# A two-layer hybrid block on one core: the later modulation tiles of layer 0 formed by TensorE in column groups

## The chip, the core and the metric

The kernel runs on one core of one Trainium2 chip. The metric is the device time of one execution in microseconds (us). The profile names the engines PE (TensorE, matmuls; PEld is its loading of weights), DVE (VectorE), ACT (ScalarE), POOL (GpSimd) and SP (SyncE, which issues all of this kernel's DMAs from one queue).

## The reference

Two layers over 512 image tokens and 256 context tokens of 1024 channels, all in float32. A condition vector c (and c_ctx for the context tokens) gives, by one matrix per layer, six vectors of 1024 channels: shift, scale and gate of the mixers, shift, scale and gate of the MLP.

```python
cond = jax.nn.silu(c)
cond_ctx = jax.nn.silu(c_ctx)
for i in range(DEPTH):
    mod = (cond @ mod_w[i] + mod_b[i])[:, None, :]
    mod_c = cond_ctx @ mod_w[i] + mod_b[i]
    sh1, sc1, g1, sh2, sc2, g2 = jnp.split(mod, 6, axis=-1)
    ...
    u = modulate(rmsnorm(h, norm1_g[i]), sh1, sc1) @ w_in[i]
    ...   # four mixers: SSD scan, differential attention, grouped-query attention, latent attention
    h = h + g1 * (jnp.concatenate([y_a, y_b, y_c, y_d], axis=-1) @ w_out[i])
    h = h + g2 * squared_relu_mlp(modulate(rmsnorm(h, norm2_g[i]), sh2, sc2), mlp_w1[i], mlp_w2[i])
    ...   # in layer 0 the same for the context tokens, with mod_c
return rmsnorm(h, final_norm_g)
```

mod_w[i] is 1024 x 6144, so a layer's modulation is 48 tiles of 128 channels, each the product of a 1024 x 128 block with two vectors.

## The kernel before

Channels lie on the partitions and tokens along the free dimension. Every large product is made of three matmuls (high by high, high by low, low by high), as activations and weights are split into exact pairs of 12-bit parts: ACT copies the high part and DVE or POOL forms the low part (`split`, L346 to L349).

The modulation is formed in two ways. Tiles 0 to 15 of layer 0 (shift and scale of the first norm) are formed at the start on PE: `mod_load` (L260 to L272) has the two condition vectors as stationary columns, padded with zeros to 32 (`sil`), and moves 256 columns of the weights past them. The eight blocks of the contraction go to four groups of 32 PSUM partitions, two blocks to a group; `mod_done` (L274) then adds the groups and turns channels onto the partitions by four matmuls against the 0/1 matrix `sel`. All later tiles, 16 to 47 of layer 0 and all 48 of layer 1, are formed on DVE by `mod_block` (L295 to L307): two loads of 128 x 512 with a column of the matrix on each partition, four (in layer 1's later tiles two) multiplies with a running sum against the condition vectors spread over all partitions (`cb`), whose product goes to `junk` and whose sum is kept (L305), and a last instruction that adds halves and bias (L307).

A layer has two stages. `mixers` (from L647) runs five tracks side by side: attention, support (all projections, then the preparation of latent attention), the SSD scan, modulation (`mods`, tiles 16 to 39 in layer 0: first gate, second shift and scale), and the first part of the out projection. A table of costs and weights (`Weave`, `TUNE`) decides which track writes its next step into the program; each engine then works off its instructions in the order that results from it. After the mixers come the rest of the out projection and the MLP, where `next_mod` hangs a tile on each of the first eight up projections (tiles 40 to 47, the MLP's gate, from `mod_now`) and later layer 1's 48 tiles.

What the change shares with the rest: the loads of weights and of modulation columns rotate through seven buffers (tag `wr`); all small PSUM results (transposes, side projections, sums) rotate through four banks (tag `g`), scores through two larger ones (`S`); the SSD scan has three buffers under the tag `sd`.

Of the kernel before, what the change touches and what calls it, by code (L numbers as in the profile page):

```python
# [19 lines left out]
P = 128  # L20
D = 1024
KT = 8
# [8 lines left out]
# columns of w_in by 128-wide tile, in the order in which the kernel names them  # L31
# [27 lines left out]
# parameter columns of a layer  # L59
# [12 lines left out]
class Weave:  # L72
    """Runs generators side by side. A track is (generator, weight); a generator yields the cost of its last
    step, or None while it cannot go on, and the track whose weighted cost is least goes next."""
# [45 lines left out]
def hybrid_block_kernel(ctx: ExitStack, tc: tile.TileContext, a: dict, out: bass.AP, dbg=None):  # L120
# [8 lines left out]
    # how the tracks of a layer are woven: costs of hops between engines and through DMA, weights, priorities  # L129
# [98 lines left out]
    # silu(c), silu(c_ctx) as zero-padded stationary columns  # L228
# [6 lines left out]
    sil = sd("sil", (P, KT, 32))  # L235
# [24 lines left out]
    def mod_load(i):  # L260
        """shift and scale of two channel tiles on TensorE, four contraction tiles side by side, for the first norm"""
        po = ps_o(f"pm{i}")
        for j in range(2):
            for k0 in range(0, KT, 3):
                n = min(3, KT - k0)
                w = mws.pop((i, j, k0))
                for k in range(k0, k0 + n):
                    g = k % 4
                    mm(po[32 * g : 32 * g + 32, 256 * j : 256 * j + 256], sil[:, k], w[:, k - k0], start=k < 4, stop=k >= 4)
        m = sd(f"ms{i}", (P, 512))  # L270
        act(m, po, AF.Copy)
        return m  # L272
# [10 lines left out]
    cb = const("cb", [P, 2, D])     # silu(c), silu(c_ctx) on every partition  # L283
# [9 lines left out]
    junk = const("junk", [P, 512], mybir.dt.bfloat16)  # L293

    def mod_block(l, c):  # L295
        """a column of mod_w on each partition"""
        L = lay[l]
        n = 2 if l + 1 < DEPTH or c < MG1 else 1
        m = tiny(f"ma{l}_{c}", 4)
        for i in range(2):  # L300
            w = sb.tile([P, 512], F32, name=f"mv{l}_{c}_{i}", tag="wr", bufs=NWR)
            half = slice(512 * i, 512 * i + 512)
            ld(w, a["modw"][l, c, :, half])
            for s in range(n):
                stt(out=junk, in0=w, scalar=1.0, in1=cb[:, s, half], op0=ALU.mult, op1=ALU.mult,  # L305
                    accum_out=m[:, 2 * i + s : 2 * i + s + 1])
        stt(out=L.mod[:, c, 0:n], in0=m[:, 0:n], scalar=col(L.v, V_MODB + c), in1=m[:, 2 : 2 + n], op0=ALU.add, op1=ALU.add)  # L307

    LO0 = nc.gpsimd.scalar_tensor_tensor
    LOP = ()  # L310

    def mod_gain(l, which, k0, k1):
        """gain * (1 + scale) for channel tiles k0..k1"""
        L = lay[l]
        off, voff = (MSC1, V_N1) if which == 1 else (MSC2, V_N2)
        key = f"gs{l}_{which}"
        if not hasattr(L, key):
            setattr(L, key, const(key, [P, KT, 2]))
        g = getattr(L, key)
        n = 2 if which == 1 or l + 1 < DEPTH else 1  # L320
        stt(out=g[:, k0:k1, 0:n], in0=L.mod[:, off + k0 : off + k1, 0:n], scalar=1.0,
            in1=L.v[:, voff + k0 : voff + k1].unsqueeze(2).to_broadcast([P, k1 - k0, n]), op0=ALU.add, op1=ALU.mult)
        return g

# [1 line left out]
    def rstd(name, srcs, parts, r):  # L326
        """srcs: (squares / count [K, tokens], 0/1 weights [K, P]) whose products add up to the mean squares.
        r <- 1 / sqrt(mean + eps) on every row that the mean is for."""
        for i, s in enumerate(parts):
            ps = ps_r(f"{name}_ms{i}")[:, 0 : s.stop - s.start]  # L330
            for j, (x, w) in enumerate(srcs):
                mm(ps, w, x[:, s], start=j == 0, stop=j == len(srcs) - 1)
            yield K.hop
            yield from rstd_of(f"{name}_q{i}", ps, r, s)

    def rstd_of(name, ps, r, s):
# [3 lines left out]
        # one Newton step  # L340
# [5 lines left out]
    def split(hi, lo, src, sub=tt):  # L346
        """fp32 -> an exact pair of 12-bit parts."""
        act(hi, src, AF.Copy)  # L348
        sub(out=lo, in0=src, in1=f(hi), op=ALU.subtract)  # L349

    def weights(name, src, m, sub=tt):
        """src: [P, k-tiles * m], a block of columns in k-tiles, or two blocks; loaded, then split by halves.
        A generator: loads, first half, second half; returns the (hi, lo) operands"""
# [19 lines left out]
    def gemm(outs, w, xs):  # L373
        """outs: (PSUM view, token slice)"""
# [8 lines left out]
    def big_gemm(name, w, xs, toks, evac, m=P):  # L383
        """x and context in one PSUM tile of two banks; evac(view, tokens)"""
        ps = ps_s(name)
        b = toks[0].start
        yield from gemm([(ps[0:m, t.start - b : t.stop - b], t) for t in toks], w, xs)
        evac(ps[0:m, 0 : toks[-1].stop - b], slice(b, toks[-1].stop))

    def side_gemm(name, w, xs, toks, evac, m=P):  # L390
        """one bank, one token range after the other"""
# [15 lines left out]
    def pump(gap):  # L407
        """a step of the deferred work, every `gap` steps"""
# [9 lines left out]
    def ahead(jobs, at=(0, 0)):  # L418
        """jobs: (weights, use); the weights of the next job are asked for before the use of this one,
        and their halves split after the steps `at` of it"""  # L420
# [41 lines left out]
    def norm_part(name, h, acc, gain, shift, si, s, xn):  # L462
        """rmsnorm over all channels, modulated, split, for the tokens s"""
# [6 lines left out]
    def squares(name, acc, k, h, s, add=gtt):  # L470
        """acc += h * h / D"""
# [7 lines left out]
    def sigmoid_of(t):  # L479
        """t <- 1/(1+exp(-t)), t >= -80"""  # L480
# [38 lines left out]
    def v_start(l):  # L519
        """V of diff and gqa, tokens on partitions"""  # L520
# [56 lines left out]
    # 0/1 matrices that add up the rows of a head: two heads of 64 rows, four of 32 rows, two of 32 + 32 rows  # L577
# [35 lines left out]
    def rope32(x, rows, name):  # L613
        """rotates 32-row groups in place on the image tokens"""
# [11 lines left out]
    def mixers(l, xn, yd, h, ys):  # L626
# [63 lines left out]
        class Unit:  # L690
            """one head and query tile on its way through the softmax"""
# [33 lines left out]
        def pv(us, vcols):  # L725
            """two heads side by side: out [(head, dim), query]"""
# [9 lines left out]
        def attend(begin, rest, middle, vcols, store, s_cost, lag=1):  # L736
            """two heads, in three stages over the (query tile, head) units: scores and softmax, transposed, times V"""
# [18 lines left out]
        def finish(i, yo):  # L756
            """parks an output until the out projection"""
# [71 lines left out]
        def gnorm(name, xs_, w, count, gains, parts):  # L829
            """xs_: (rows, tile)"""  # L830
# [160 lines left out]
        def ssd_dt():  # L991
# [3 lines left out]
            dts = mid(f"dts{l}", 48, 7)   # softplus(dt + bias)  [token, (d, t, h)]  # L995
# [8 lines left out]
            # log1p(e) = 2 atanh(e / (2 + e)), e = exp(-|x|)  # L1004
# [28 lines left out]
            wst = mid(f"wst{l}", 48, 7)   # dt * exp(acs_end - acs)  # L1033
# [5 lines left out]
            nb = mid(f"nb{l}", 48, 7)     # ln(dt) - acs  # L1039
# [5 lines left out]
        def conv(name, i):  # L1045
            """centred convolution of width 3 from PSUM, silu"""
# [159 lines left out]
        def modjobs():  # L1206
            if l == 0:
                for c in range(MG1, MG2):
                    yield c

# [24 lines left out]
        def mods():  # L1235
            for c in modjobs():
                mod_block(l, c)
                yield K.w_m
            done.add("mods")

# [34 lines left out]
    for l in range(DEPTH):  # L1275
# [24 lines left out]
        def out2_jobs(si, s):  # L1300
            """the contraction tiles of mla, four output tiles at a time"""
# [15 lines left out]
        mod_now = iter(range(MG2, 48) if l == 0 else ())  # L1317
        mod_next = iter(range(48) if l + 1 < DEPTH else ())

        def next_mod(g):  # L1320
            if g == 0:
                c = next(mod_now, None)
                if c is not None:
                    mod_block(l, c)
# [103 lines left out]
def _layout(i):  # L1428
    """The inputs as the kernel loads them: copies and permutations only."""
    i = {n: np.asarray(v) for n, v in i.items()}  # L1430

    def cols(v):            # channels -> [P, tiles]
        return v.reshape(-1, P).T

    def rep(v):             # one row on every partition
        return np.broadcast_to(v.reshape(1, -1), (P, v.size))

    def ktiles(w):          # [K, n] -> [P, k-tiles, n]
        return w.reshape(-1, P, w.shape[1]).transpose(1, 0, 2)

    def blocks(w):          # [1024, n * P] -> [n, P, KT * P]
# [18 lines left out]
    for l in range(DEPTH):  # L1460
# [10 lines left out]
         "rope": _rope_tables(), "win": np.stack(win), "wv": np.stack(wv), "modw": np.stack(modw), "mod0": i["mod_w"][0][:, 0 : 2 * D].reshape(KT, P, 2, 4, 256).transpose(3, 2, 1, 0, 4),  # L1471
# [19 lines left out]
```

## Time and profile before

| | us |
|---|---|
| median of 3 runs (1855.38 to 1856.95) | 1855.81 |
| span of the profiled execution, first to last instruction | 1851.9 |
| PE busy | 1743.4 |
| DVE busy | 1188.5 |
| ACT busy | 870.0 |
| POOL busy | 536.6 |

The page gives the busy time of each engine over the whole span, 29429 instructions. It is an average over stages with different limits: the start (to about 56 us), layer 0's mixers (to about 460), its out projection and MLP (to about 1093), and the same for layer 1. The rows below are therefore taken by stretches of the span. Busy time of PE runs to the modelled end of each matmul, so matmuls that stand alone take more of it than matmuls in a dense row.

### The profile page before, as it was taken

The page shows a single profiled execution, that of the slowest core. Times are in us where ns is not written, and L with a number is a line of the kernel's source. Part 1 is how long each engine was busy: PE and PEld are TensorE (multiplying, and loading weights), DVE is VectorE, ACT ScalarE, POOL GpSimd, SP SyncE. Part 2 cuts the span into 40 slices and gives each one's busy share as a digit, 9 for nine tenths or more (in the row PEclk, how much of TensorE's full clock was granted, in tenths as well). Part 3 has the DMA queues.
Part 4 walks back from the last instruction along what each step waited for, and adds up shares of the span by engine and source line. Part 5 has one row for each costly group of instructions (what it writes and reads, how often), then busy time and mean ns, then how long its engine had stood idle before and what let it go on. Part 6 is the DMA issues. An engine that isn't in the chain of part 4 may idle for free.

```text
span 1851.9 us, 29429 instructions
## 1 busy us (share of the span) xinstructions
PE 1743.4 (94%) x10686; PEld 1467.2 (79%) x10686; DVE 1188.5 (64%) x2352; ACT 870.0 (47%) x1768; POOL 536.6 (29%) x477
## 2 busy tenths in 40 slices
PE   7979888899988999999999999998999999999996
PEld 5967677677777988888888889786778998888885
DVE  5799998877499964543543164877976863333324
ACT  5345656777354313213213353676877752323242
POOL 2443552220235201001002664465211320101065
PEclk9989899999999999999999999999999999999998
DMA  8465331013344642442433434422014552323233
GB/s 329 128 177 170 91 103 39 10 52 142 96 143 148 199 131 93 146 132 92 150 123 95 135 113 121 128 73 66 13 48 161 169 162 95 97 92 98 94 121 98
DMA packets 117328, 216.23 MB, mean 117 GB/s; under 512 B 15424, under 2 KB 24640, under 8 KB 117184
## 3 DMA queue, kind: packets, MB, share of 16 engines
q1 hardware_dynamic: 117184, 214.36, 37.4%
q8 instruction: 84, 1.38, 0.3%
q14 instruction: 60, 0.49, 0.1%
HBM read 185.99 MB, written 8.13 MB: 105 GB/s over the span
## 4 chain that ended last, share of the span: by engine, by line
PE 64%; DVE 17%; issue 5%; POOL 4%; ACT 4%; DMA 3%; SPq 3%; DVEq 0%; POOLq 0%; ACTq 0%
PE p L380 41%; DVE junk L305 4%; PE po L380 3%; SPq L673 2%; PE pv L530 2%; PE pr L380 2%; PE m_s L701 2%; PE m_o L732 2%; PE m_t L722 1%; DMA mv<-in_modw_dram 1%; DVE d_m L706 1%; POOL w_512s L349 1%; DVE d_p L785 1%; PE pdk L380 1%; DVE hs L1116 1%
## 5 line engine op out<-in xcount | busy, mean ns | idle before, releaser
L348 ACT ACTIVATE w_0s<-w 128x512 fp32r<-128x512 f32 x256 | 160.8, 630 | 389.8 <-PE p L380 370.3
L305 DVE SCALAR_TENSOR_TENSOR junk<-mv,cb 128x512 bf16<-128x512 f32 x256 | 200.9, 785 | 129.0 <-DMA mv<-in_modw_dram 126.4
L1345 POOL TENSOR_TENSOR r<-r 128x512 f32<-128x512 f32 (+2 forms) x80 | 92.0, 1152 | 648.8 <-ACT a_0h L1344 310.5
L349 DVE TENSOR_TENSOR w_0s<-w,w_0s 128x512 fp32r<-128x512 f32 x216 | 151.5, 703 | 158.2 <-ACT w_0s L348 157.9
L1269 DVE SCALAR_TENSOR_TENSOR h<-p,modT,h 128x512 f32<-128x512 f32 (+1 forms) x104 | 62.6, 623 | 101.1 <-PE p L380 101.1
L1343 ACT ACTIVATE r<-p 128x512 f32<-128x512 f32 (+2 forms) x80 | 47.7, 596 | 156.5 <-PE p L380 153.8
L710 ACT ACTIVATE d_p<-d_s,d_m 128x768 f32<-128x768 f32 (+1 forms) x80 | 65.0, 815 | 66.5 <-DVE d_m L706 62.5
L779 POOL TENSOR_TENSOR d_p<-d_p,d_m 128x768 f32<-128x768 f32 (+1 forms) x40 | 59.1, 1478 | 85.8 <-DVE d_m L714 83.7
L706 DVE TENSOR_REDUCE d_m<-d_s 128x1 f32<-128x768 f32 (+1 forms) x80 | 66.0, 840 | 4.6 <-PE d_s L701 4.4
L349 POOL TENSOR_TENSOR w_0s<-w,w_0s 128x512 fp32r<-128x512 f32 x40 | 55.1, 1388 | 41.0 <-ACT w_0s L348 37.9
L477 POOL TENSOR_TENSOR acc<-acc,sq 128x256 f32<-128x256 f32 (+1 forms) x48 | 49.2, 1026 | 46.4 <-ACT sq L476 40.3
L701 PE MATMUL d_s<-sdk,sdq 128*128 128x256 f32 (+1 forms) x144 | 43.7, 391 | 18.5 <-ACT d_p L710 12.0
L380 PE MATMUL p<-xm_0h,w_0s 128*128 128x512 f32 (+1 forms) x176 | 54.4, 355 | 2.5 <-ACT r L1343 2.2
L380 PE MATMUL p<-a_0h,w_0s 128*128 128x512 f32 (+1 forms) x176 | 54.4, 355 | 0.9 <-DVE h L1269 0.5
L380 PE MATMUL p<-xm_4h,w_0s 128*128 128x512 f32 (+1 forms) x176 | 54.4, 356 | 0.5 <-DVE w_0s L349 0.5
L380 PE MATMUL p<-xm_5h,w_0s 128*128 128x512 f32 (+1 forms) x176 | 54.4, 355 | 0.0
L380 PE MATMUL p<-xm_3h,w_0s 128*128 128x512 f32 (+1 forms) x176 | 54.4, 355 | 0.0
L380 PE MATMUL p<-a_4h,w_0s 128*128 128x512 f32 (+1 forms) x176 | 54.4, 354 | 0.0
L380 PE MATMUL p<-xm_2h,w_0s 128*128 128x512 f32 (+1 forms) x176 | 54.4, 355 | 0.0
L380 PE MATMUL p<-xm_1h,w_0s 128*128 128x512 f32 (+1 forms) x176 | 54.3, 355 | 0.0
L380 PE MATMUL p<-xm_6h,w_0s 128*128 128x512 f32 (+1 forms) x176 | 54.3, 355 | 0.0
L380 PE MATMUL p<-a_2h,w_0s 128*128 128x512 f32 (+1 forms) x176 | 54.1, 354 | 0.0
(2374 smaller groups left out, 5659.4 us busy)
## 6 DMA issues: line engine op xcount, KB each, us to landing
w<-in_w_dram SPq DMA_DIRECT2D x320, 256.0 KB, 2.7
mv<-in_modw_dram SPq DMA_DIRECT2D x160, 256.0 KB, 2.9
wr<-in_wout_dram SPq DMA_DIRECT2D x32, 256.0 KB, 2.8
h<-in_xT_dram SPq DMA_DIRECT2D x16, 384.0 KB, 6.9
mw<-in_mod_dram SPq DMA_DIRECT2D x16, 384.0 KB, 6.1
wo<-in_wout_dram SPq DMA_DIRECT2D x32, 192.0 KB, 2.5
wv<-in_wv_dram SPq DMA_DIRECT2D x16, 192.0 KB, 4.7
y<-yd SPq DMA_DIRECT2D x6, 384.0 KB, 4.0
```

The costliest lines, as they stand in the source:

```text
L305: stt(out=junk, in0=w, scalar=1.0, in1=cb[:, s, half], op0=ALU.mult, op1=ALU.mult, accum_out=m[:, 2 * i + s : 2 * i + s + 1])
L348: act(hi, src, AF.Copy)
L349: sub(out=lo, in0=src, in1=f(hi), op=ALU.subtract)
L380: mm(o, w[k][wi], xs[k][xi][0:r, t], start=k == 0 and wi == 0 and xi == 0, stop=k == n - 1 and wi == 1)
L477: (tt if k == KT - 1 else add)(out=acc[:, s], in0=acc[:, s], in1=q[:, s], op=ALU.add)
L701: mm(u.ps[:, b:e_], q[:, P * t : P * t + P], k[:, u.k0 + b : u.k0 + e_], start=i == 0, stop=i == len(passes) - 1)
L706: nc.vector.tensor_reduce(out=u.m[:, 0:1], in_=u.ps[:, 0 : u.n], axis=AX.X, op=ALU.max, negate=True)
L710: act(u.p, u.ps[:, 0 : u.n], AF.Exp, bias=u.m[:, 0:1], accum_out=u.m[:, 1:2])
L779: gtt(out=a.p, in0=a.p, in1=a.r.to_broadcast([P, n]), op=ALU.mult)
L1269: stt(out=h[k][:, s], in0=ps, scalar=L.mod[:, mg + k, si : si + 1], in1=h[k][:, s], op0=ALU.mult, op1=ALU.add)
L1343: act(r, ps, AF.Relu)
L1345: gtt(out=r, in0=r, in1=r, op=ALU.mult)
```

## The change

The 32 later tiles of layer 0 are formed on PE as the first 16 are, four tiles at a time (`mod_quad`). A tile is two loads (the same 2 x 256 KB, another layout of the same numbers), eight matmul calls with 32 stationary and 128 moving columns into four groups of partitions of one small PSUM bank, and one copy by ACT; after four tiles four matmuls against `sel` add the groups, and one DVE instruction adds the bias for the four. `sil` gets a buffer of its own, as it now lives on; `junk` moves to the ring `sc` of two buffers. Layer 1's tiles stay with `mod_block`.

```diff
-    sil = sd("sil", (P, KT, 32))
+    sil = const("sil", [P, KT, 32])
...
-    junk = const("junk", [P, 512], mybir.dt.bfloat16)
...
+        junk = sb.tile([P, 512], mybir.dt.bfloat16, name=f"junk{l}_{c}", tag="sc", bufs=NSC)
...
+    def mod_quad(c0):
+
+        L = lay[0]
+        m = sd(f"mq{c0}", (P, 512))
+        for j in range(4):
+            ws = []
+            for i in range(2):
+                w = sb.tile([P, 4, P], F32, name=f"mk{c0 + j}_{i}", tag="wr", bufs=NWR)
+                ld(w, a["modk"][c0 + j - MG1, :, 4 * i : 4 * i + 4])
+                ws.append(w)
+            po = ps_g(f"pk{c0 + j}")
+            for k in range(KT):
+                g = k % 4
+                mm(po[32 * g : 32 * g + 32, 0:P], sil[:, k], ws[k // 4][:, g], start=k < 4, stop=k >= 4)
+            act(m[:, P * j : P * j + P], po[:, 0:P], AF.Copy)
+            yield K.w_m
+        pq = ps_g(f"pl{c0}")
+        for j in range(4):
+            mm(pq[:, 2 * j : 2 * j + 2], m[:, P * j : P * j + P], sel, start=True, stop=True)
+        tt(out=L.mod[:, c0 : c0 + 4], in0=pq[:, 0:8].rearrange("p (k s) -> p k s", s=2),
+           in1=L.v[:, V_MODB + c0 : V_MODB + c0 + 4].unsqueeze(2).to_broadcast([P, 4, 2]), op=ALU.add)
...
         def mods():
-            for c in modjobs():
-                mod_block(l, c)
-                yield K.w_m
+            if l == 0:
+                for c in range(MG1, MG2, 4):
+                    yield from mod_quad(c)
             done.add("mods")
...
-        mod_now = iter(range(MG2, 48) if l == 0 else ())
+        mod_now = (x for c in ((MG2, MG2 + 4) if l == 0 else ()) for x in mod_quad(c))
...
             if g == 0:
-                c = next(mod_now, None)
-                if c is not None:
-                    mod_block(l, c)
+                next(mod_now, None)
```

The order of the instructions follows from the tracks, so some of it moves. On DVE, where differential attention's first units begin (d_..._m are the row maxima and sums of a unit, dq the rotated queries), there stood before:

```order
L714 RECIPROCAL d_0_0_1_0_m<-d_0_0_1_0_m 128x1 [waits Activation_49]
L305 SCALAR_TENSOR_TENSOR junk,ma_21_988<-mv_21_1_993,cb 128x512 [waits DMAHW7_49]
L706 TENSOR_REDUCE d_0_0_1_1_m<-d_0_0_1_1_s 128x1 [waits PE_49]
L706 TENSOR_REDUCE d_0_1_0_0_m<-d_0_1_0_0_s 128x1 [waits PE_49]
L621 TENSOR_TENSOR dq_1106<-dq_1106,rddq_1_1195 128x512 [waits DVE_49,Pool_49]
L305 SCALAR_TENSOR_TENSOR junk,ma_21_988<-mv_21_1_993,cb 128x512 [waits DVE_49]
L714 RECIPROCAL d_0_0_1_1_m<-d_0_0_1_1_m 128x1 [waits Activation_49]
```

Now the same place has the unit's work alone:

```order
L735 RECIPROCAL d_0_0_1_0_m<-d_0_0_1_0_m 128x1 [waits Activation_49]
L727 TENSOR_REDUCE d_0_1_0_0_m<-d_0_1_0_0_s 128x1 [waits PE_49]
L642 TENSOR_TENSOR dq_1141<-dq_1141,rddq_1_1230 128x512 [waits DVE_49,Pool_49]
L806 SCALAR_TENSOR_TENSOR d_0_0_0_0_p<-d_0_0_0_1_p,d_0_0_0_1_m,d_0_0_0_0_p 128x768 [waits DMAHW5_49,DMAHW1_49,DVE_49]
L735 RECIPROCAL d_0_0_1_1_m<-d_0_0_1_1_m 128x1 [waits Activation_49]
```

On PE, behind the first projection (pdk) and ahead of the second (pdq), the tiles 16 and 17 now stand (pk; mk are their loads):

```order
L401 MATMUL pdk_676<-xn_7h,wdk00s_669 128x256
L321 MATMUL pk_688<-mk_0_684,sil 32x128 [waits DMAHW6_49,DVE_49]
L321 MATMUL pk_688<-mk_0_684,sil 32x128 x3
L321 MATMUL pk_688<-mk_1_686,sil 32x128 [waits DMAHW7_49]
L321 MATMUL pk_688<-mk_1_686,sil 32x128 x3
L321 MATMUL pk_729<-mk_0_725,sil 32x128 [waits DMAHW0_49,DVE_49]
L401 MATMUL pdq_0_766<-xn_0h,wdq00s_710 128x512 [waits Activation_49]
```

Before, pdq followed pdk directly. The first call of tile 17 stands ahead of the 24 matmuls of pdq_0, its other seven behind them; the first call of each tile waits for its load and for its PSUM bank.

On SP's queue, the load of tile 20 stood ahead of the 16 copies that stack the heads of dk (sdk):

```order
L303 DMA mv_20_0_898<-in_modw_dram 128x512 [waits DMAHW4_49,DVE_49]
L303 DMA mv_20_1_902<-in_modw_dram 128x512 [waits DMAHW5_49,DMAHW3_49,DVE_49]
L360 DMA wgk_0_977<-in_win_dram 128x512 [waits Pool_49]
L360 DMA wgk_1_979<-in_win_dram 128x512 [waits DMAHW6_49,DVE_49]
L303 DMA mv_21_0_989<-in_modw_dram 128x512 [waits DMAHW7_49,DVE_49]
L673 DMA sdk_0_0_0_823<-hldk_0h 32x768 [waits Activation_49]
```

Now it stands behind them:

```order
L694 DMA sdk_0_1_1_850<-hldk_0l 32x768 [waits DMAHW0_49]
L694 DMA sdk_0_1_1_850<-hldk_0l 32x768 [waits DMAHW1_49]
L316 DMA mk_0_920<-in_modk_dram 128x512 [waits DMAHW2_49,PE_49]
L316 DMA mk_1_922<-in_modk_dram 128x512 [waits DMAHW3_49,PE_49]
L694 DMA sdq_0_0_0_962<-hldq_0h 32x768 [waits DMAHW4_49,Activation_49]
```

The tile's load has moved behind the 16 copies, and it now waits for PE to free its buffer, where it waited for DVE.

## Rows read from the trace of the kernel before

**Rows 1.** The page, part 1: busy us (share of the span) x instructions.
```profile
PE 1743.4 (94%) x10686; PEld 1467.2 (79%) x10686; DVE 1188.5 (64%) x2352; ACT 870.0 (47%) x1768; POOL 536.6 (29%) x477
```

**Rows 2.** By stretch: length; busy PE, PEld, DVE, ACT, POOL; clock; DMA share, GB/s.
```profile
56.00:330.00 274.00, 240.20 (x1495) 195.70 (x1495) 252.64 (x567) 149.85 (x334) 117.29 (x100) 0.94 0.41 117
100.00:150.00 50.00, 42.55 (x241) 35.24 (x242) 48.73 (x100) 27.49 (x59) 21.87 (x14) 0.86 0.67 187
200.00:250.00 50.00, 39.66 (x238) 33.19 (x239) 48.40 (x103) 30.25 (x67) 24.94 (x25) 0.86 0.35 101
...
510.00:600.00 90.00, 79.61 (x451) 66.57 (x449) 85.78 (x153) 46.83 (x91) 35.27 (x27) 1.00 0.47 148
600.00:1035.00 435.00, 433.40 (x2491) 380.37 (x2491) 223.71 (x489) 109.37 (x174) 61.09 (x46) 1.00 0.40 128
1100.00:1410.00 310.00, 294.32 (x2008) 239.39 (x2008) 238.71 (x454) 206.86 (x447) 120.05 (x104) 0.99 0.28 75
```

**Rows 3.** Chain of waits, 56 to 330 us, shares by line.
```profile
by line: DVE junk L305 18.3%; SPq L673 11.4%; issue 10.5%; DVE d_m L706 5.8%; DVE d_p L785 5.0%; DVE hs L1116 2.5%; DVE modT L307 2.3%; PE pst L1102 1.5%; PE pz L380 1.3%; DMA r<-in_rope_dram 1.3%; PE d_o L732 1.2%; PE pe L1139 1.1%; ACT d_
```

**Rows 4.** Chain of waits, 510 to 600 us, shares by line.
```profile
by line: DVE junk L305 21.6%; issue 21.0%; DVE n_t L458 9.8%; PE pr L380 7.9%; DVE w_0s L349 7.0%; DVE w_512s L349 2.6%; DVE h L1269 2.3%; DVE modT L307 2.2%; DVE xm_3l L460 1.9%; DVE a_6l L1346 1.9%; DVE xm_4l L460 1.7%; DVE a_4l L1346 1.6
```

**Rows 5.** Busy time by stretch: junk (L305), then modT (L307).
```profile
56.00:330.00 274.00, 83.61 (x192) 0.94 0.41 117
510.00:600.00 90.00, 26.75 (x64) 1.00 0.47 148
...
56.00:330.00 274.00, 11.12 (x24) 0.94 0.41 117
510.00:600.00 90.00, 2.62 (x8) 1.00 0.47 148
```

**Rows 6.** Waits of ACT, 56 to 330 us: in total, times, longest.
```profile
ACT d_p L710 <- DVE d_m L706: 50.9, 23, 7.1
```

**Rows 7.** Waits of SP's queue, 510 to 600 us: in total, times, longest.
```profile
SPq L303 <- DVE junk L305: 13.9, 7, 3.1
SPq L360 <- DVE junk L305: 12.6, 7, 3.3
```

**Rows 8.** Timeline of PE: start, us from start to end, instruction.
```profile
16.24 0.63 PE L269 MATMUL pm<-mw,sil 128*32 128x256 f32 x6
16.80 1.56 PE L500 MATMUL n_ms<-sq,ones 128*128 128x512 f32 x4
...
33.70 0.34 PE L530 MATMUL pvb<-wv_0s,xn_1h 128*128 128x384 f32 x1
33.87 0.34 PE L530 MATMUL pvb<-wv_0s,xn_1l 128*128 128x384 f32 x1
34.14 1.93 PE L269 MATMUL pm<-mw,sil 128*32 128x256 f32 x32
36.00 0.62 PE L530 MATMUL pv<-wv_1s,xn_2h 128*128 128x384 f32 x2
...
39.27 0.95 PE L277 MATMUL pn<-sel,ms 128*128 128x2 f32 x8
40.08 0.42 PE L530 MATMUL pv<-wv_1s,xn_3h 128*128 128x384 f32 x1
```

**Rows 9.** Groups of ACT, 56 to 460 us: count | busy, mean ns | idle.
```profile
L820 ACT ACTIVATE yg<-g_o 128x128 f32<-128x128 f32 x12 | 3.4, 280 | 1.8 <-PE g_o L732 1.7
```

**Rows 10.** Groups of PE, 56 to 330 us, then 1100 to 1410 us.
```profile
L732 PE MATMUL d_o<-d_pt,dv 128*64 128x128 f32 x224 | 18.7, 297 | 1.9 <-ACT d_pt L723 1.1 <-DVE cvxs L1057 0.8
L701 PE MATMUL d_s<-sdk,sdq 128*128 128x512 f32 x32 | 16.7, 529 | 14.2 <-ACT d_p L710 7.8 <-DMA sdq<-hldq_0l 6.4
...
L701 PE MATMUL d_s<-sdk,sdq 128*128 128x512 f32 x64 | 18.5, 379 | 2.9 <-ACT d_p L710 2.8
...
L732 PE MATMUL d_o<-d_pt,dv 128*64 128x128 f32 x192 | 13.3, 278 | 1.2 <-ACT d_pt L723 1.2
```

**Rows 11.** Waits of DVE, 600 to 1035 us: in total, times, longest.
```profile
DVE junk L305 <- DMA mv<-in_modw_dram: 126.4, 72, 3.7
```

More of the change, by code (lines that the diff above doesn't have):

```diff
@@ L690, in mixers @@
         class Unit:
+            pass
         def scores(name, passes, t):
@@ L1204, in gproj @@
             return proj(n, toks, ev, how, after)
[L1206 to L1209, printed above, removed]
         def support():
@@ L1470, in _layout @@
     d = {"par": np.concatenate(par, axis=1), "xT": ktiles(np.concatenate([i["x"][0], i["ctx"][0]], axis=0).T),
-         "rope": _rope_tables(), "win": np.stack(win), "wv": np.stack(wv), "modw": np.stack(modw), "mod0": i["mod_w"][0][:, 0 : 2 * D].reshape(KT, P, 2, 4, 256).transpose(3, 2, 1, 0, 4),
+         "rope": _rope_tables(), "win": np.stack(win), "wv": np.stack(wv), "modw": np.stack(modw), "modk": blocks(i["mod_w"][0][:, P * MG1 :]).reshape(-1, P, KT, P), "mod0": i["mod_w"][0][:, 0 : 2 * D].reshape(KT, P, 2, 4, 256).transpose(3, 2, 1, 0, 4),
          "wout": np.stack(wout), "wout2": i["w_out"][:, 768:].reshape(DEPTH, 2, P, D), "w1": np.stack(w1), "w2": np.stack(w2), "wuq": np.stack(wuq), "wukv": np.stack(wukv)}
```

## The prediction

> **What bounds the kernel now.** I read the page first, then the busy time by stretch, then the chain of waits in the two stretches in which the change has its work, then the groups of instructions there. The page says that PE is busy for 94% of the span and DVE for 64% [rows 1]; on that alone, work that moves from DVE to PE is a loss. By stretch it looks different [rows 2]. From 56 to 330 us (layer 0's mixers while 24 of the 32 tiles are formed) DVE is busy for 252.6 of 274 us and PE for 240.2; from 510 to 600 us (start of layer 0's MLP, the other 8 tiles) DVE for 85.8 of 90 and PE for 79.6. From 600 to 1035 us PE is busy for 433.4 of 435 us. So DVE is the fuller engine in just the two stretches that the change touches, and PE elsewhere. The chain says the same: in the first stretch the multiply-and-sum (junk, L305) has 18.3% of it and the sum with the bias (modT, L307) 2.3%, together 56 us; PE lines come far behind [rows 3]. In the second stretch the two have 23.8%, 21 us [rows 4].
>
> **What DVE loses.** In the first stretch L305 takes 83.6 us in 192 records (24 tiles, 4 multiplies each, and a read of the sum behind each) and L307 11.1 us; in the second 26.8 and 2.6 us [rows 5]. DVE falls from 252.6 to about 158 of 274 us, and from 85.8 to 56 of 90. What waited for it: ScalarE's exponentials stood 50.9 us for row maxima that came late from DVE [rows 6], and in the MLP the loads of weights and of modulation columns stood 26.5 us in SP's queue until a multiply freed one of the 7 load buffers [rows 7]. Now PE frees these buffers as soon as it has passed over them.
>
> **What PE gets, per tile.** The start of the kernel already has this form (pm, L269): column groups of 32, moving 256 columns where the new ones move 128. The profile shows each call as two records. 32 records: the last matmul ahead starts at 33.87, its neighbours follow 0.18 apart, so the next would have come at 34.05; the next after the group comes at 36.00 [rows 8]. So 32 records cost 1.95 us. 6 records, in two rounds of up to four groups, cost 0.56 us from their start to the next start (16.24 to 16.80), 32 in eight rounds 1.86 [rows 8]: (1.86 - 0.56) / 6 = 0.217 us per round, and 0.13 us that does not depend on the length, with 0.09 us ahead: 0.22 us for each change to column groups and back. A tile has 16 records, four rounds. Bounds: at half the columns a round is 0.108 us and a tile 4 x 0.108 + 0.22 = 0.65 us; if a round stays as long as with 256 columns, 4 x 0.217 + 0.22 = 1.09 us. Nothing speaks for the longer round but the weight load, so I start from 0.65; but in the built order about half of the tiles are cut in two by other matmuls (one call, then up to 24 matmuls of a projection, then the other seven), which is a second change (0.22) and a round for itself. I take **0.85 us** per tile.
>
> **Per four tiles** there is the addition of the groups (pl, 4 calls). The same at the start (pn) takes from 39.27 to the next matmul at 40.08, 0.81 us [rows 8]. The Trainium skill ("TensorEngine Tiling (Array Packing)", section Instruction Overhead) says that a matmul with one column costs the same as one with 60, about 60 cycles. At 2.4 GHz that would be 25 ns a record as an estimate from that page, 0.2 us per four tiles; the row shows four times that, so the row is used, and by the page the sum would come out 5 us lower.
>
> PE gets 24 x 0.85 + 6 x 0.81 = **25 us** in the first stretch and 8 x 0.85 + 2 x 0.81 = **8 us** in the second. ScalarE gets 32 copies of 128x128 out of PSUM at 0.28 us [rows 9], 9 us on an engine that is busy for 150 of the 274; DVE gets 8 small additions. Both lie beside other work; if ScalarE is late with a copy, that is the rival below. Layer 1's 48 tiles stay on DVE: the spread condition vectors and their 16 matmuls are still needed, so nothing is taken off PE. DMA moves the same bytes in the same 2 x 256 KB. The scratch of layer 1's multiplies now comes from a ring of two; DVE writes it alone and in order, so I cost it at nothing.
>
> **First stretch.** Is there room on PE for 25 us? The busy time of 240.2 us is not all work. Score matmuls of 512 columns (d_s) cost 16.7 / 32 = 0.52 us of busy time here and 18.5 / 64 = 0.29 in layer 1's mixers, where no modulation is on DVE; the products with V (d_o) 18.7 / 224 = 0.083 against 13.3 / 192 = 0.069 [rows 10]. Lone matmuls, and the stretches around 100 to 150 and 200 to 250 us where the granted clock averages 0.86 [rows 2] (so 28% of each at the lower level, 1.2 GHz, after idle time of PE), fill busy time without work. These two groups, 15% of the busy time, hold 7.4 + 3.2 = 10.6 us of that; I take 15 for all. That leaves 225 us, with the new work 250. Layer 1's mixers, the same code without modulation, keep PE busy for 294.3 of 310 us, 0.949 [rows 2]. 250 / 0.949 = 264 us in place of 274: **-10 us**. Bounds: if all 240 us are work, 265 / 0.949 = 280, **+6**; if PE became dense, 250, **-24**.
>
> **Second stretch.** 79.6 + 8 = 87.6 us of work, and PE at the share that it has right after, 433.4 / 435: 88 us in place of 90, **-2 us** (bounds: 0, if the split of weights and of the second norm on DVE still holds PE back; -8, if part of its busy time here is empty too). What follows at 600 us is PE's alone and moves along.
>
> The sum is 12 us. The profiled execution has a span of 1851.9 us; the median of the runs, 1855.8, is 3.9 us longer, what lies around the span, and the change does not touch that. 1855.8 - 12 = **1844 us**.
>
> **Rivals.**
> *PE stands at the new matmuls (slower).* What DVE took late, at nobody's cost but its own, is now in PE's order, and all projections and scores are queued behind. The first matmul of each tile waits for its load and for one of the four small PSUM banks, which scores, transposes and side projections share; the bank comes free when ScalarE or DVE has copied it. For it: later, in the MLP, DVE did wait for these loads, 126.4 us in 72 waits, 1.8 us each [rows 11]; and the load of the fifth tile now stands behind 16 copies on SP's queue. Against it: in the first stretch no wait of DVE for these loads is among those the profile lists, and PE releases their buffers earlier. The Trainium skill (the same page, section PSUM Bottleneck) warns that tiling speeds up TensorE but not the emptying of PSUM; here a copy (0.28 us) is shorter than its tile, which speaks against it so far. Price: at 1 us per tile, 32 - 12 = +20, 1876 us. It decides from 12 / 32 = 0.38 us per tile on. Chance 0.12.
> *PE has no room (slightly slower).* The busy time was all work: +6 - 2 = +4, 1860 us. Against it are rows 10. Chance 0.09.
> *The softmax chain only changes its bottleneck (no change).* Behind L305 the chain lists SP's copies of stacked heads (L673, 11.4%), issue (10.5%) and the maxima themselves (5.8%) [rows 3]; if these and POOL's products hold the pace, the gain just pays for the PE work: 1852 to 1859. Chance 0.14.
> *The chain gives back nearly all.* 56 us off the chain less 25 us of PE work would be -31, but PE's 250 us of work are a floor: -24, and -2 to -8 in the MLP: about 1827. Chance 0.17.
> That the multiplies stay is ruled out by the built order: DVE has them for layer 1 alone.
>
> **The numbers.** My forecast, a gain of 4 to 20 us, has 0.48, its time is 1844. With the larger gain, faster by over 0.2% (3.7 us, about what a measurement of this kernel can tell) gets 0.65; within it 0.14; slower 0.21. The range goes from 1826, where PE is dense, to 1862, beyond the case without room; left out are most of the waiting PE (0.09) and the far end of the large gain.
>
> **What would show it.** In the profile after: a tile's 16 records at 0.65 to 0.85 us from the last matmul ahead to the next; DVE near 158 us in a mixers' stretch of about 264 us with the granted clock above 0.94; PE at 0.93 to 0.96 there; the waits of d_p for d_m below half; no multiply waiting in SP's rows of the MLP's start. I am wrong if PE's idle time is listed against pk with loads or ScalarE as releaser and comes to over 12 us, or if PE is as idle as before with POOL, ScalarE or SP as releaser.

## The result, and the profile after

The changed kernel takes 1867.3 us (median of 4 runs, 1866.4 to 1869.2) against 1856.4 for the kernel before in the same runs: ratio 1.0056, 95% interval 1.0042 to 1.0069. It is 11 us slower, where 12 us faster was forecast. The profiled execution (1869.2 us) has a span of 1867.5 us.

The page, part 1 (as [rows 1]):

```profile
PE 1784.5 (96%) x11262; PEld 1494.1 (80%) x11262; DVE 1074.7 (58%) x2072; ACT 879.2 (47%) x1800; POOL 521.8 (28%) x477
```

DVE has lost 114 us and PE has gained 41. The forecast had 33 us of new work on PE and 15 us of its busy time gone, so 18.

By stretch, with the columns of [rows 2]. The first row goes from 56 us to the point that lay at 330 us before: the last product of differential attention with V ended at 299.1 us, and now ends at 311.9, so the stretch ends 30.9 us behind it, at 342.8.

```profile
56.00:342.80 286.80, 268.48 (x1932) 212.60 (x1930) 170.71 (x360) 158.19 (x361) 106.44 (x102) 0.95 0.39 112
...
100.00:150.00 50.00, 43.60 (x286) 32.42 (x286) 28.96 (x51) 26.98 (x59) 19.07 (x14) 0.86 0.61 172
...
510.00:600.00 90.00, 86.04 (x550) 70.10 (x549) 61.40 (x86) 48.86 (x94) 36.04 (x29) 1.00 0.46 145
```

The same work takes 286.8 us instead of 274, while DVE is busy for only 171 us of it. PE, 240 us busy before, is now busy for 268. In the chain of waits of this stretch no DVE line stands near the top any more:

```profile
by line: PE pxs L401 6.5%; PE d_o L753 6.4%; PE pk L321 5.0%; PE pdk L401 5.0%; PE pz L401 4.8%; PE pdq L401 4.6%; PE d_t L743 4.3%; PE d_s L722 3.7%; PE pcqx L401 3.3%; SPq L694 3.2%; PE pgk L401 3.1%; PE pcq L401 3.1%; PE pc L401 3.0%; PE
```

The waits of PE, DVE and ACT in it (in total, times, longest), one engine after the other:

```profile
PE pk L321 <- DMA mk<-in_modk_dram: 6.7, 3, 2.6
PE d_s L722 <- ACT d_p L731: 4.7, 6, 1.1
...
DVE d_m L727 <- PE d_s L722: 30.6, 16, 5.7
...
ACT d_p L731 <- DVE d_m L727: 11.9, 10, 3.9
```

The wait of ACT for row maxima fell from 50.9 us [rows 6] to 11.9, as intended. But now DVE waits for PE's scores, 30.6 us, and the chain is made of PE's lines: PE sets the pace here. Two pieces of PE's timeline (start, us from start to end) show what a tile costs. The first is tile 19's end, an addition, and tile 20's first call; the second a tile cut in two by three transposes.

```profile
86.87 0.40 PE L401 MATMUL pdk<-xn_7h,wdk10s 128*128 128x512 f32 x1
87.20 0.64 PE L321 MATMUL pk<-mk,sil 128*32 128x128 f32 x14
87.76 1.06 PE L326 MATMUL pl<-sel,mq 128*128 128x2 f32 x8
91.38 0.38 PE L321 MATMUL pk<-mk,sil 128*32 128x128 f32 x2 [2.56 <-DMA mk<-in_modk_dram]
91.69 0.46 PE L401 MATMUL pdk<-xn_0h,wdk10s 128*128 128x256 f32 x1
```

```profile
264.52 0.41 PE L321 MATMUL pk<-mk,sil 128*32 128x128 f32 x2
264.85 0.55 PE L743 MATMUL d_t<-ident,d_p 128*128 128x128 f32 x3
265.33 0.64 PE L321 MATMUL pk<-mk,sil 128*32 128x128 f32 x14
265.90 0.66 PE L743 MATMUL d_t<-ident,d_p 128*128 128x128 f32 x4
```

One call of a tile (2 records) holds the row for 264.85 - 264.52 = 0.33 us, the other seven (14 records) for 0.57. The 16 records of a whole tile hold it for 0.57 too (86.11 to 86.68 in the timeline of e5, below). So in a cut tile the first call comes on top, at more than half the price of a tile.

### The profile page after: what moved, and what is told of

It is laid out like the page before. It is cut to its first block, busy times and chain, and to the rows that moved or that the text cites. A ratio compares the mean times of both kernels' runs of the same rounds, so it can differ in the third digit from the quotient of the medians.

```text
span 1867.5 us, 30324 instructions
## 1 busy us (share of the span) xinstructions
PE 1784.5 (96%) x11262; PEld 1494.1 (80%) x11262; DVE 1074.7 (58%) x2072; ACT 879.2 (47%) x1800; POOL 521.8 (28%) x477
## 4 chain that ended last, share of the span: by engine, by line
PE 80%; DVE 8%; ACT 4%; POOL 4%; issue 3%; DMA 1%; SPq 1%; DVEq 0%; POOLq 0%; ACTq 0%
PE p L401 45%; PE po L401 3%; PE pv L551 2%; PE pxs L401 2%; PE pdk L401 2%; PE pr L401 2%; PE m_s L722 2%; PE m_o L753 2%; PE d_o L753 1%; PE pdq L401 1%; PE m_t L743 1%; PE pk L321 1%; PE pcqx L401 1%; PE pgk L401 1%; PE d_t L743 1%
## 5 line engine op out<-in xcount | busy, mean ns | idle before, releaser
L304 DVE SCALAR_TENSOR_TENSOR junk<-mv,cb 128x512 bf16<-128x512 f32 x128 | 91.6, 719 | 116.3 <-DMA mv<-in_modw_dram 115.2
L800 POOL TENSOR_TENSOR d_p<-d_p,d_m 128x768 f32<-128x768 f32 (+1 forms) x40 | 55.1, 1378 | 107.0 <-DVE d_m L735 102.9
L401 PE MATMUL p<-xm_7h,w_0s 128*128 128x512 f32 (+1 forms) x176 | 54.4, 357 | 0.0
L401 PE MATMUL p<-a_6h,w_0s 128*128 128x512 f32 (+1 forms) x176 | 54.3, 355 | 0.0
```

Source lines behind the costliest of these rows:

```text
L401: mm(o, w[k][wi], xs[k][xi][0:r, t], start=k == 0 and wi == 0 and xi == 0, stop=k == n - 1 and wi == 1)
L800: gtt(out=a.p, in0=a.p, in1=a.r.to_broadcast([P, n]), op=ALU.mult)
```

## The experiments

Each was timed against the kernel before, which was at 1855.8 to 1856.8 us each time; the brackets are 95% intervals of the ratio. Two theories to begin with: **W**, PE had no room, its new work is paid in full; **S**, PE stands for loads at the new matmuls.

**Which part loses.** First the MLP's tiles alone on PE (e1), then the mixers' alone (e2), the others by the old `mod_block`:

```diff
 # e1, in mods()
-                for c in range(MG1, MG2, 4):
-                    yield from mod_quad(c)
+                for c in range(MG1, MG2):
+                    mod_block(l, c)
+                    yield K.w_m
 # e2
-        mod_now = (x for c in ((MG2, MG2 + 4) if l == 0 else ()) for x in mod_quad(c))
+        mod_now = (mod_block(0, c) for c in (range(MG2, 48) if l == 0 else ()))
```

> Only the MLP's 8 tiles are formed on PE; the mixers' 24 stay on DVE. Both theories (W: the new PE work is paid nearly in full, as PE had no room in the mixers; S: PE stands there for loads) put the whole loss into the mixers. The milestones of the two traces (the mixers' part ends 15 us later, layer 1 starts 11 us later) then give a gain of about 5 us in the MLP: 1851 us against 1856 before, and the mixers' last SSD product (pe) ends at 395 us as before. A third view, that the gain after 510 us came from something other than the 8 tiles, gives 1856.

> The reverse: the mixers' 24 tiles on PE, the MLP's 8 on DVE. W and S: the mixers end 15 us later and nothing is given back, 1871 to 1872 us. If the two parts do not add (the later start of the MLP hides its DVE work), about 1867.

Measured: e1 1855.7 us, ratio 0.9998 [0.9989, 1.0006]; e2 1867.9 us, 1.0063 [1.0049, 1.0078]. The whole loss lies in the mixers' 24 tiles. The MLP's 8 gain nothing (my 5 us, read from two single executions, were wrong), though PE's busy time from 510 to 600 us rose as forecast (87.2 us in e1, 87.6 forecast).

**What is the relief worth, and what the price?** e3 leaves the mixers' tiles out; e4 keeps all matmuls but replaces the loaded operand by a resident one:

```diff
 # e3, in mods()
-                for c in range(MG1, MG2, 4):
-                    yield from mod_quad(c)
+                nc.vector.tensor_copy(L.mod[:, MG1:MG2], L.v[:, V_MODB + MG1 : V_MODB + MG2]...)
 # e4, in mod_quad
-                w = sb.tile([P, 4, P], F32, name=f"mk{c0 + j}_{i}", tag="wr", bufs=NWR)
-                ld(w, a["modk"][c0 + j - MG1, :, 4 * i : 4 * i + 4])
-                ws.append(w)
+                ws.append(cb[:, i, 0 : 4 * P].rearrange("p (g q) -> p g q", q=P))
```

> The mixers' 24 tiles are left out altogether (their modulation is the bias alone; nothing is loaded, multiplied or copied for them); the MLP's 8 are on PE. It shows what the relief of DVE gives when PE pays nothing. W: the tiles and their additions cost PE some 25 us (24 x 0.85 + 6 x 0.81), all of it paid, so 1867 - 25 = 1842 us, and the relief was worth about 10 us next to 1851. If the softmax chain was never held by DVE's multiplies, 1850 to 1852, and the price of a tile on PE is 16 / 24 = 0.67 us or less. If my prediction's size of the relief was right (PE near 225 us of work at 0.949, 237 us in place of 274), about 1815 to 1820.

> All 32 tiles are formed by the same matmuls at the same places of PE's order, but the moving operand is a resident tile: nothing is loaded for them, no buffer is taken, and no first call waits for a load. S: the waits of pk for loads (6.7 us in 3 waits of the trace) and what SP's queue holds up go away, 1856 to 1860 us. W: a wait of PE only moved work that PE did later anyway, 1864 to 1867 us.

Measured: e3 1836.6 us, 0.9898 [0.9881, 0.9915]; e4 1864.5 us, 1.0043 [1.0029, 1.0057]. From e1 to e3 the relief of DVE, with the tiles' loads gone too, is worth 19 us, half of what I forecast (274 - 225 / 0.949 = 37). From e3 to the changed kernel PE's work costs 31 us, 28 of them without any load. S falls as the main cause. The stretch of e3 up to the same point, and its score and V products by form (busy us, mean ns):

```profile
56.00:309.30 253.30, 234.79 (x1497) 194.12 (x1496) 166.75 (x352) 150.49 (x336) 106.30 (x101) 0.97 0.29 76
```

```profile
L753 PE MATMUL d_o<-d_pt,dv 128*64 128x128 f32 x224 | 19.9, 286 | 0.0
L722 PE MATMUL d_s<-sdk,sdq 128*128 128x512 f32 x32 | 15.7, 494 | 9.5 <-ACT d_p L731 8.1 <-DMA sdq<-hldq_0l 1.4
```

With DVE relieved and no tile on PE, PE is still busy for 234.8 us, only 5.4 less than before, and the two groups of products together take what they took: 35.6 us against 35.4 [rows 10].

**Cut tiles.** In the changed kernel the mixers' 24 tiles stand in 35 pieces on PE. e5 sets the track's offset in the order to 0, which brings the calls together (26 pieces); e9 leaves the track where it was and ties calls 2 to 8 to the first (24 pieces); e10 is e5 with the resident operand of e4:

```diff
 # e5
-... a_o=-51, a_m=-58
+... a_o=-51, a_m=0
 # e9, in mod_quad
-                mm(po[32 * g : 32 * g + 32, 0:P], ...)
+                with tc.high_priority(400 if k else 1):
+                    mm(po[32 * g : 32 * g + 32, 0:P], ...)
```

> Only the order of the modulation track changes (its priority offset in layer 0 from -58 to 0): the eight calls of a tile stand together on PE, where in the changed kernel 12 tiles are cut in two. If a cut costs what the trace of the changed kernel shows for one (0.5 us for the first call alone), 10 cuts in the mixers are 4 to 5 us: 1862 to 1863 us against 1867. If PE's price is the matmuls alone and the cuts lie beside other waits, 1866 to 1868.

> The track stays where it was (offset -58), but calls 2 to 8 of a tile get a high priority, so that they follow the first at once: the cuts go, the late place of the tiles and most of their loads' places stay. The trace of the changed kernel has 9 more pieces in the mixers than the kernel of the third experiment's successor (calls together) at some 0.55 us each, and 6.7 us of waits for loads. If the cuts are the loss: 1855 to 1858 us. If the waits for loads are: 1861 to 1865. If it is the place of the whole track in the order: 1865 to 1868.

> Calls together and nothing loaded for the 32 tiles (a resident operand). With the cuts gone, what the loads cost is the difference to the kernel with calls together (1855.6). Its trace shows no wait of PE for a modulation load, so 1854 to 1856 us; if loads still hold up SP's queue or the buffers of the projections' weights, 1851 to 1853. Without the mixers' tiles the time was 1836.6: 18 us for the calls alone is 24 x 0.55 and 6 x 0.85.

Measured: e5 1855.6 us, 0.9994 [0.9985, 1.0003]; e9 1853.3 us, 0.9991 [0.9981, 1.0002]; e10 1858.0 us, 1.0009 [1.0000, 1.0018]. Keeping a tile's calls together takes the whole loss away, at either place of the track (more than I expected of either; two tiles even stay cut in e5). Without cuts no cost of the loads shows: e10 lies 2 us above e5 and above both of its expectations. The stretch of e5, and a tile in its timeline:

```profile
56.00:326.80 270.80, 256.64 (x1926) 205.37 (x1924) 167.51 (x359) 157.19 (x360) 107.90 (x102) 0.97 0.41 118
```

```profile
85.23 0.95 PE L326 MATMUL pl<-sel,mq 128*128 128x2 f32 x8
86.11 0.64 PE L321 MATMUL pk<-mk,sil 128*32 128x128 f32 x16
86.68 0.50 PE L401 MATMUL pdk<-xn_6h,wdk10s 128*128 128x512 f32 x1
```

The waits for loads went with the cuts. In the changed kernel SP's queue issued both halves of tile 20's load at 88.46 us, behind the 16 copies (sdk); in e9 the first half went out at 72.85 and the second at 86.45, and PE's waits for the tiles' loads fell from 6.7 to 1.1 us:

```profile
71.10 0.81 SPq L316 DMA_DIRECT2D mk<-in_modk_dram  x2
...
87.14 1.22 SPq L694 DMA_DIRECT2D sdk<-hldk_0l  x2
88.46 1.02 SPq L316 DMA_DIRECT2D mk<-in_modk_dram  x2
```

```profile
70.50 0.80 SPq L316 DMA_DIRECT2D mk<-in_modk_dram  x2
72.85 0.33 SPq L316 DMA_DIRECT2D mk<-in_modk_dram  x1
86.45 0.53 SPq L316 DMA_DIRECT2D mk<-in_modk_dram  x1
```

**More cuts.** The same suspect, made larger: e5 (and e10, for e13) with calls 2 to 8 set back.

```diff
-                mm(po[32 * g : 32 * g + 32, 0:P], ...)
+                with tc.high_priority(-24 if k else 1):
+                    mm(po[32 * g : 32 * g + 32, 0:P], ...)
```

> The kernel with calls together (26 pieces of modulation matmuls on PE in the mixers, 1855.6 us), with calls 2 to 8 of each tile set back by 24 places in the priority: 50 pieces, 24 more. The changed kernel has 35, 9 more, and takes 11.7 us more. If a cut costs its own second change to column groups and nothing else (0.55 us): 24 x 0.55 = 13, 1869 us. If it costs as much again through loads that come late behind it (11.7 / 9 = 1.3 us): 24 x 1.3 = 31, 1887 us. If cuts cost nothing and it is the place of the track that counts: 1854 to 1858.

> The same cuts without loads (a resident operand): 49 pieces against 28 in the kernel with calls together and no loads (1858.0 us), 21 more. Own price alone: 21 x 0.55 = 12, 1869 to 1870 us, whichever of the first two holds with loads. Below 1862: what a cut costs is its loads.

Measured: e12 1880.4 us, 1.0123 [1.0108, 1.0137], 24.8 more than e5, 1.03 per added piece; e13 1875.4 us, 1.0102 [1.0087, 1.0116], 17.4 more than e10, 0.83 per added piece. In the MLP 8 (e12) and 6 (e13) pieces are added as well, which this count leaves out; with them it is 0.78 and 0.64 us. e12 lies between its expectations, e13 5 us above its own. So most of a cut's price in these two runs is there without any load. A cut in e13:

```profile
79.65 0.28 PE L400 MATMUL pdq<-xn_1h,wdq00s 128*128 128x256 f32 x1
79.77 0.28 PE L400 MATMUL pdq<-xn_1l,wdq00s 128*128 128x256 f32 x1
79.98 0.41 PE L320 MATMUL pk<-cb,sil 128*32 128x128 f32 x2
80.32 0.38 PE L400 MATMUL pdq<-xn_1h,wdq00s 128*128 128x256 f32 x1
80.63 0.63 PE L320 MATMUL pk<-cb,sil 128*32 128x128 f32 x12
81.19 0.39 PE L400 MATMUL pdq<-xn_2h,wdq00s 128*128 128x256 f32 x1
```

From 79.77 to 80.32 a single call takes 0.55 us, where these matmuls follow each other at 0.12: 0.43 us for one call of eight. The six calls behind it hold the row for 0.56 us (12 records). A whole tile between the same projections costs, by the same measure, 79.48 - 78.70 - 0.12 = 0.66 us (e5):

```profile
78.70 0.28 PE L401 MATMUL pdq<-xn_3h,wdq00s 128*128 128x256 f32 x1
78.91 0.65 PE L321 MATMUL pk<-mk,sil 128*32 128x128 f32 x16
79.48 0.39 PE L401 MATMUL pdq<-xn_4h,wdq00s 128*128 128x256 f32 x1
```

As seven calls hold the row as long as eight, a cut's own price on PE's row is the 0.43 us of the lone call. Two more rows show what is in it. In the changed kernel four calls, one in each column group, hold the row for 0.36 us, hardly longer than the lone call with its 0.33; and in e5 a lone call of an addition (pl), which uses the whole array, adds only 591.17 - 590.91 - 0.12 = 0.14 us:

```profile
146.47 0.43 PE L321 MATMUL pk<-mk,sil 128*32 128x128 f32 x8
146.83 0.61 PE L722 MATMUL d_s<-sdk,sdq 128*128 128x512 f32 x2
```

```profile
590.91 0.28 PE L401 MATMUL p<-xm_0l,w_512s 128*128 128x256 f32 x1
591.03 0.28 PE L326 MATMUL pl<-sel,mq 128*128 128x2 f32 x2
591.17 0.37 PE L401 MATMUL p<-xm_0h,w_512s 128*128 128x256 f32 x1
```

So a lone call takes the two rounds (0.22 us, by the prediction's 0.108 each) in which four could have run side by side, and about 0.21 us more for the change to column groups and back. The Trainium skill ("TensorEngine Tiling (Array Packing)", section Tiling Modes, Key Properties) says that changing the tiling mode drains TensorE. The rows agree as far as a change has a price; they do not show the drain itself.

The row does not hold all of a cut's price. In e13 27 added pieces at 0.43 are 12 of 17.4 us, in the changed kernel 9 against e5 are 4 of 11.7. The stretches of these two executions take 286.8 and 270.8 us. Of the 16 us between them, longer idle time of PE is 4 (18.3 against 14.2 us), and the granted clock (0.95 and 0.97) up to 6, as an estimate: 0.05 x 286.8 = 14 us lost against 0.03 x 270.8 = 8. What of this follows from the cuts, and how, was not run apart.

**Half, and other orders.** e7 leaves 12 of the mixers' tiles out and has all others on DVE, at offset -58; e8 has those 12 on PE in pairs, at offset 0; e11 is DVE alone, as before, with the offset 0 of e5.

```diff
 # e7, e8, in mods(), by turns of four tiles
+                for c in range(MG1, MG2, 8):
+                    for e in range(c, c + 4):
+                        mod_block(l, e)
+                        yield K.w_m
 # e7
+                    yield 4 * K.w_m
 # e8
+                    yield from mod_quad(c + 4)
```

> 12 of the mixers' 24 tiles are left out (their modulation is the bias alone), 12 stay on DVE, as do the MLP's 8: how the relief of DVE grows. All 24 left out gave 19 us. In proportion: 1846 us. If DVE only holds PE back while it is full, the first half gives most of it: 1840 to 1842. If the chain needs DVE to be nearly empty: 1851.

> 12 tiles of the mixers on DVE and 12 on PE in pairs, by turns of four; the MLP's 8 on DVE. PE's price is half of that of the 12 pairs, 9 us. With a relief in proportion (9.5 us): 1855 to 1856, level with before. If the first half of the relief gives most (14 us or more): 1850 to 1851, faster than both kernels.

> All 32 tiles on DVE as before, but the modulation track's offset is 0 instead of -58: does that number help by itself? If the offset only decides about cuts on PE, it does nothing here: 1855 to 1857 us. If multiplies that come ahead in DVE's order hold up the row maxima (the kernel with half of the tiles on DVE and this offset was at 1864.9): 1862 to 1870. If it is a better order whatever the engine: 1845 to 1850.

Measured: e7 1848.7 us, 0.9961 [0.9949, 0.9973]; e8 1864.9 us, 1.0046 [1.0033, 1.0059]; e11 1866.0 us, 1.0061 [1.0044, 1.0078]. Half of the relief gives 7 us, the other half 12; by the intervals (5 to 9.5 us for the half, 16 to 22 for all) an even split is not ruled out. The offset 0 costs multiplies on DVE 10 us and saves matmuls on PE 12, there by joining calls: with the calls tied, -58 is as good (e9). e8 lies 9 us above its expectations; that its DVE blocks stand at offset 0 may be why, but was not run apart.

**A faster version.** e6 puts two tiles in a row into one PSUM bank, with one copy and with loads a step ahead, at offset 0; e14 is e6 at offset -58 with its calls tied together.

```diff
 # e6, in mod_quad
+        for j0 in (0, 2):
+            wp = [loads(j0), loads(j0 + 1)]
+            yield K.w_m
+            po = ps_g(f"pk{c0 + j0}")
+            for j in range(2):
+                for k in range(KT):
+                    g = k % 4
+                    mm(po[32 * g : 32 * g + 32, P * j : P * j + P], sil[:, k], wp[j][k // 4][:, g], start=k < 4, stop=k >= 4)
+            act(m[:, P * j0 : P * j0 + 2 * P], po[:, 0 : 2 * P], AF.Copy)
+            yield K.w_m
```

> Two tiles in a row into one PSUM bank, one copy for both, loads issued one step ahead of the matmuls, calls kept together. If the price on PE is calls plus changes to column groups, two tiles take 8 rounds of 0.108 plus one change of 0.22, 1.08 us, so 12 pairs 13 us and 6 additions 5 us: 18 us over the kernel without the mixers' tiles (1836.6), that is 1855 us, level with before. If a tile costs as much in a pair as alone (the price is something else, such as PE's order), 1862 to 1865.

> The two best edits in one: two tiles in a row with their loads a step ahead (1851.7 us), and the track back at its place (-58) with calls 2 to 16 held to the first (1853.3 us for single tiles). Half of the changes to column groups go, 12 x 0.22 = 2.6 us: 1850 to 1851. If the pair's gain was the place and not the pairing: 1853 to 1855.

Measured: e6 1851.7 us, 0.9975 [0.9965, 0.9984]; e14 1854.6 us, 0.9990 [0.9980, 0.9999]. Pairs at offset 0 are the fastest complete version, 4 us under the kernel before. That e14 does not add to it speaks for the place and the earlier loads as much as for the pairing; this stays open.

## Why the prediction was wrong

The forecast for the first stretch was (225 + 25) / 0.949 = 264 us (263 without rounding up); it took 268.5 / 0.936 = 286.8. Term by term:

- **225 us of real work: the step that failed most.** I took 15 us of PE's busy time for empty, by comparing score and V products with layer 1's [rows 10], and 7.4 of them came from a misread row: layer 1's row of 64 score matmuls names only the shape of 512 columns, but holds 32 of 512 and 32 of 256. Kept apart, from the trace of before, 1100 to 1410 us:

```profile
L701 PE MATMUL d_s<-sdk,sdq 128*128 128x512 f32 x32 | 14.9, 470 | 2.9 <-ACT d_p L710 2.8
L701 PE MATMUL d_s<-sdk,sdq 128*128 128x256 f32 x32 | 9.2, 287 | 0.0
```

  So 32 matmuls of 512 columns cost 14.9 us there and 16.7 in layer 0: 1.8 us, not 7.4, and with the 3.2 of the V products 5.0, not 10.6 (the step from there to 15 had no row). e3 shows 234.8 us with DVE relieved, 5.4 less than the 240.2 of before. That these two agree is luck in part: the 5.4 did not come from the two groups, which take as long in e3 as before; why layer 1's are cheaper stays open (the granted clock differs too, 0.99 against 0.94 [rows 2]). With 235 in the sum, the stretch would have been (235 + 25) / 0.949 = 274 us, no gain. This is 9.8 us of work, 10 of the 23 us missed, and it is the rival "PE has no room", to which I gave 0.09.
- **25 us for the tiles: 33.7 (268.5 - 234.8).** The price of a whole tile was right: e5 pays 256.6 - 234.8 = 21.8 us for 24 tiles and 6 additions, where 24 x 0.65 + 6 x 0.81 = 20.5. So was the 5 us for cuts (24 x 0.20), as far as PE's row goes: 9 to 11 more pieces at 0.43 are 4 to 5 us. What the sum had at nothing is the rest of a cut's price: the changed kernel pays 11.7 us (to e5) to 14 us (to e9) for them.
- **The share 0.949**: 0.936. PE stood 6.7 us for loads, the rival "PE stands at the new matmuls" at half the 12 us from which it was to decide, but that is not what lowered the share: without any load (e4) it is 262.0 / 281.1 = 0.932, with 1.1 us of such waits (e9) 0.936, and without any tile (e3) 234.8 / 253.3 = 0.927. Layer 1's share was not this stretch's; e5 comes to it with 0.948. ScalarE's copies of the tiles were not late: no wait of PE for them is listed, only one of 0.2 us at pk for another copy. The Trainium skill ("TensorEngine Tiling (Array Packing)", section PSUM Bottleneck) says that the copy out of PSUM may become the bottleneck; here it did not. The stretches of e4 and e9:

```profile
56.00:337.10 281.10, 261.96 (x1930) 207.67 (x1928) 167.47 (x360) 156.69 (x361) 111.73 (x102) 0.97 0.26 69
56.00:333.40 277.40, 259.75 (x1929) 207.34 (x1927) 167.42 (x360) 156.73 (x361) 109.91 (x102) 0.96 0.40 115
```

- **Relief of DVE.** Right in its mechanism (DVE 171 of 287 us; ACT's wait for maxima under a half), wrong in its worth: 19 us (e1 to e3) where 37 were in the sum. DVE was to fall to 158 us; even without any tile (e3) it has 167, as the records of its lines overlap and their busy times do not subtract.
- **Second stretch**: -2 forecast; e1 has 0, with an interval from -2.0 to +1.1 us.
- **Signs.** The clock was 0.95, above 0.94 as forecast, but the stretch from 100 to 150 us stayed at 0.86. Neither of the two signs by which I meant to see myself wrong appeared (PE idle at pk for 6.7 us; PE not as idle as before): PE was busy with work, and I had named no sign for that.

So the loss is relief (-19), tiles whole (+19), cuts with all that comes with them (+12). The first two and the whole of the third are measured; how the third divides is not.

## What to carry to other kernels

Before work is moved to an engine that is nearly full, leave it out once: that run gives the most the move can bring, and here it was half of what the busy times promised. Before the means of two groups are compared, keep their shapes apart: a row can mix two and name one. Calls that change the form of TensorE's array belong together; look in the built order for groups that the scheduler has cut, and tie them (12 to 14 us here). An order constant tuned for work on one engine has to be tried again for the same work on another.

## What the runs showed that I had not expected

One call of eight, alone between projections, costs 0.43 us of PE's row, two thirds of a whole tile (0.66). Half of the tiles off DVE gives 7 us, all of them 19, so the first half did not give most of it. And taking away 64 loads of 256 KB did not make the kernel faster (1858.0 against 1855.6 us).
